# Split matmuls of a decoder layer with the moving columns and the PSUM columns taken in descending order

## The chip, the cores and the metric

The kernel runs on one core of one Trainium2 chip. The metric is the device time of one execution in microseconds. The kernel before was run three times: 1579.78, 1580.56 and 1582.54 us, median 1580.56 us. The profile is of one further execution.

## What is computed

One layer of a hybrid decoder, for 256 prompt tokens and 8 single-token samples together (264 columns), model width 2048, feed-forward width 5632:

```python
def layer(x, ...):
    xn = rmsnorm(x, g_mix)
    z = xn @ w_in                                  # 2048 x 5128
    y_rg = ...                                     # causal conv, gated linear recurrence
    y_ml = ...                                     # chunked mLSTM, 4 heads
    x = x + jnp.concatenate([y_rg, y_ml], axis=-1) @ w_out
    xq = (rmsnorm(x, g_xa) @ w_xa_q).reshape(B, L, XA_HEADS, XA_DH)
    s = jnp.einsum('blhd,bmhd->bhlm', xq, mk) * (XA_DH ** -0.5)
    p = jax.nn.softmax(s, axis=-1)
    o = jnp.einsum('bhlm,bmhd->blhd', p, mv).reshape(B, L, D_MODEL)
    x = x + o @ w_xa_o
    xf = rmsnorm(x, g_ffn)
    x = x + (jax.nn.silu(xf @ w_ffn_gate) * (xf @ w_ffn_up)) @ w_ffn_down
    return x
```

The memory keys and values `mk`, `mv` come from `rmsnorm(mem) @ w_xa_k` and `@ w_xa_v` for the prompt (256 memory tokens) and from a cache for the samples. All inputs and outputs are fp32. Beside the tokens' outputs the new recurrent states and the prompt's memory keys and values are returned.

## The kernel before

Activations stand transposed: 128 features on the partitions, 264 tokens along the free dimension, 16 chunks of 128 features for the model width. Every projection is cut into **steps** (the list `steps`). A step takes one weight piece of 128 x 2048 fp32 (1 MB), makes one output block of 128 features x 264 tokens and, in the common case, runs over 16 chunks of the contraction.

To get fp32 accuracy from a single pass, each fp32 operand is split into two tiles of type fp32r: a high part (ScalarE copies and so rounds it) and a low part (VectorE subtracts the high part from the original). The weights are split so in `split_half`, half a piece at a time, into tiles `wh` and `wl`; the activations are split once, when they are made, into two tiles out of the pool `B`. `mm3` then makes a product as the sum of three matmuls into the same PSUM bank: high weight by high activation, high weight by low activation, low weight by high activation. A matmul's second argument is the stationary operand (128 columns), the third the moving operand, whose columns stream through the array; the first is the PSUM output.

`mm3` is called at six places:

- `proj`: 16 (12 in the last part of the down projection) calls a step; n is 264, or 256 for the memory keys.
- `pe_first`: the first four pieces of `w_in`, into four banks at a time, 264 columns.
- `pe_o`: the output projection of the cross attention, 264 columns (two lines of it, 1108 to 1118).
- `attend`: scores (line 1046) and weighted values (line 1079) of the prompt's cross attention, 256 columns, in banks with the tag `ax`.

Other matmuls do not go through `mm3` and stay as they are: `pe_v` (the memory values, 512 columns, the memory activations stationary and the weights moving), the plain fp32 matmuls of the recurrence and the mLSTM, the sums over tokens, the spreading of a factor over the partitions, and the transposes.

PSUM has four banks with the tag `mm` and four with the tag `ax`, each 512 fp32 wide; an output takes columns 0 to 263 (or 0 to 255) of its bank, and a moving operand is a contiguous row of 264 (or 256) fp32 in its tile.

The order of the work: the main loop goes through the steps, issues the DMA of the piece three steps ahead (SyncE queue), the split of the piece one step ahead, the step's matmuls, and then as much of the side work (recurrence, mLSTM, attention, norms) as its own price list says will fit. A tile scheduler places the semaphore waits. Between writes of TensorE itself to one PSUM bank it also sets waits of TensorE on its own semaphore where it sees need.

Of the kernel before, what the change touches and what calls it, by code (L numbers as in the profile page):

```python
# [80 lines left out]
def layer_kernel(ctx: ExitStack, tc, xT, memT, vec, wrg, w_in, w_out, w_q, w_k, w_v, w_o,  # L81
# [92 lines left out]

    def mm3(ps, a, b, start, stop):
        ah, al = a
        bh, bl = b
        pe.matmul(ps, ah, bh, start=start, stop=False)
        pe.matmul(ps, ah, bl, start=False, stop=False)
        pe.matmul(ps, al, bh, start=False, stop=stop)  # L180
# [609 lines left out]
    def proj(src, rhs, evac, cols=2048, n=N, need=()):  # L790

        def f(i):
            ps = bank()
            w = W(i)
            nch = cols // P
            for c in range(nch):
                mm3(ps[:, :n], w(c), rhs(c), c == 0, c == nch - 1)
            return ps
        steps.append((src, cols, f, evac, need))
# [5 lines left out]
    def pe_first(q):  # L805
        def f(i):
            w = W(i)
            for n in range(4):
                for c in range(4):
                    mm3(first[n][:, :N], w(4 * n + c), rx(4 * q + c), q + c == 0, q + c == 6)  # L810
        return f
# [220 lines left out]
    def attend(h):  # L1032
# [9 lines left out]
        for tb in range(2):  # L1042
            ps = bank("ax")
            s = slice(tb * P, tb * P + P)
            for c in range(4):
                mm3(ps[:, :T], (qh[:, c, s], ql[:, c, s]), K(c), c == 0, c == 3)
            yield STEP
            mx, su = sm[:, 2 * tb: 2 * tb + 1], sm[:, 2 * tb + 1: 2 * tb + 2]
            dve.tensor_reduce(mx, ps[:, :T], axis=AX.X, op=OP.max)
            dve.tensor_scalar(mx, mx, -XSCALE, None, op0=OP.mult)  # L1050
            act.activation(p[:, tb, :], ps[:, :T], AF.Exp, scale=XSCALE, bias=mx, accum_out=su)
            yield 0.5
# [147 lines left out]
    for i, (src, cols, pef, evf, need) in enumerate(steps):  # L1200
# [17 lines left out]
        ps = pef(i)  # L1218
# [127 lines left out]
```

## Time and profile before

| what | value |
|---|---|
| runs, median of three | 1580.56 us (1579.78 to 1582.54) |
| profiled execution, span from first to last instruction | 1577.6 us |
| median less span | 2.96 us |
| TensorE (PE) busy | 1560.9 us, 99%, 12356 matmuls |
| weight load (PEld) busy | 1536.0 us, 97%, 12356 loads |
| VectorE (DVE) busy | 1047.3 us, 66% |
| ScalarE (ACT) busy | 779.2 us, 49% |
| GpSimd (POOL) busy | 74.9 us, 5% |
| DMA | 325.97 MB, mean 207 GB/s |
| TensorE's mean granted clock | 0.994 of full speed |

The profile gives no separate time of its execution, only the span, so the span is what a sum is made against; the median of the runs lies 2.96 us above it. The line number of nearly all instructions is that of a helper (line 60), so groups are told apart by tile names and shapes: `mm<-B,wh 128x264` is a matmul into a bank with the tag `mm`, with an activation tile of pool `B` moving and the high half of the weights stationary. The time that the profile gives for one matmul contains its way through the array, and neighbours overlap; how often matmuls start is read from their number in a stretch of time.

### The profile page before, as it was taken

To read this page: it belongs to the slowest core of one execution; us is meant where nothing else is said; L and a number is where in the kernel's file an instruction comes from. 1 tells how busy PE (TensorE), PEld (TensorE's weight loads), DVE (VectorE), ACT (ScalarE), POOL (GpSimd) and SP (SyncE) were. 2 spreads that over 40 slices of the span, in tenths; PEclk is the share of its full clock that TensorE was granted. 3 is DMA by queue.
4 is the path that set the end of the run, shared out by engine and by line. 5 is a ranking of instruction groups with operands and counts; after the bars stand their busy time and mean duration, and the time that the engine had idled before them with its cause. 6 is when DMAs were issued, how large, how long until landed. Compare 5 with 4: busy or idle time off the path is not lost.

```text
span 1577.6 us, 29752 instructions
## 1 busy us (share of the span) xinstructions
PE 1560.9 (99%) x12356; PEld 1536.0 (97%) x12356; DVE 1047.3 (66%) x2019; ACT 779.2 (49%) x1217; POOL 74.9 (5%) x142
## 2 busy tenths in 40 slices
PE   9999999999999999999999999999999999999997
PEld 9999999999999889989999999999999999999997
DVE  7976878787689999856655555455555554555554
ACT  7465775564445555545444444333444433344463
POOL 0001210001012112000000000000000000000000
PEclk9999999999999999999999999999999999999999
DMA  8445875547689888554545555455445555555452
GB/s 311 154 174 171 303 262 202 189 159 260 247 298 353 314 330 302 178 182 180 187 163 185 188 181 173 182 187 186 174 178 185 188 181 174 180 188 188 153 180 97
DMA packets 55303, 325.97 MB, mean 207 GB/s; under 512 B 6688, under 2 KB 7120, under 8 KB 24448
## 3 DMA queue, kind: packets, MB, share of 16 engines
q1 hardware_dynamic: 39744, 270.68, 47.9%
q0 software_dynamic: 15136, 53.16, 9.2%
q8 instruction: 96, 1.57, 0.4%
q10 hardware_dynamic: 288, 0.23, 0.1%
q14 instruction: 39, 0.32, 0.1%
HBM read 312.78 MB, written 11.28 MB: 205 GB/s over the span
## 4 chain that ended last, share of the span: by engine, by line
PE 97%; ACT 1%; DVE 1%; DMA 0%; issue 0%; SPq 0%; DVEq 0%; ACTq 0%
PE mm L60 92%; PE ax L60 6%; DVE B L60 1%; ACT B L60 1%; DMA xres<-xT 0%; ACT wh L60 0%; ACT L60 0%; DVE wl L60 0%; DVE c L60 0%; DVEq L1323 0%; DVE xres L60 0%; ACT t L60 0%; SPq L1185 0%; ACT rstd L60 0%; SPq L1178 0%
## 5 line engine op out<-in xcount | busy, mean ns | idle before, releaser
L60 PE MATMUL mm<-B,wh 128*128 128x264 f32 (+1 forms) x7520 | 1380.0, 285 | 2.8 <-DVE B L60 2.8
L60 PEld LDWEIGHTS mm<-B,wh 128*128 128x128 f32 x7520 | 1166.8, 189 | 4.4 <-ACT cso L60 2.9
L60 PE MATMUL mm<-B,wl 128*128 128x264 f32 (+1 forms) x3760 | 1066.9, 284 | 1.2 <-DVE wl L60 1.2
L60 ACT ACTIVATE wh<-raw 128x1024 fp32r<-128x1024 f32 (+2 forms) x518 | 538.4, 1041 | 710.1 <-PE mm L60 584.1
L60 DVE TENSOR_TENSOR wl<-raw,wh 128x1024 fp32r<-128x1024 f32 (+2 forms) x518 | 620.7, 1200 | 370.0 <-ACT wh L60 361.8
L60 PEld LDWEIGHTS mm<-B,wl 128*128 128x128 f32 x3760 | 708.8, 189 | 1.6 <-DVE wl L60 1.4
L60 DVE TENSOR_TENSOR t<-mm,rstd 128x264 f32<-128x264 f32 x104 | 44.9, 432 | 57.5 <-PE mm L60 57.5
L60 PE MATMUL mm<-wh,B 128*128 128x512 f32 x256 | 83.0, 398 | 0.0
L60 DVE TENSOR_TENSOR xres<-xres,mm 128x264 f32<-128x264 f32 x80 | 34.3, 428 | 46.5 <-PE mm L60 46.5
L60 PEld LDWEIGHTS mm<-wh,B 128*128 128x128 f32 x256 | 48.4, 189 | 10.5
L60 DVE SCALAR_TENSOR_TENSOR dw<-B,dw 128x256 f32<-128x256 f32 x128 | 53.8, 420 | 3.2 <-ACT dw L60 2.2
L60 PE MATMUL mm<-wl,B 128*128 128x512 f32 x128 | 51.0, 398 | 0.0
L60 PE MATMUL ax<-B,B 128*128 128x256 f32 (+3 forms) x288 | 48.7, 312 | 0.0
L60 DVE SCALAR_TENSOR_TENSOR dw<-B,qsm,dw 128x256 f32<-128x256 f32 x96 | 45.9, 480 | 1.2 <-ACT dw L60 0.6
L60 PEld LDWEIGHTS ax<-B,B 128*128 128x128 f32 x288 | 40.7, 189 | 3.4 <-issue 0.7
L1238 POOL TENSOR_TENSOR B<-B,rstd 128x264 f32<-128x264 f32 x4 | 2.8, 739 | 866.0 <-ACT rstd L60 866.0
L60 ACT ACTIVATE B<-xres,vecs 128x264 fp32r<-128x264 f32 (+1 forms) x64 | 31.2, 504 | 2.5 <-DMA xres<-xT 1.3
L60 ACT ACTIVATE t<-xres 128x264 f32<-128x264 f32 x60 | 23.8, 416 | 15.3 <-DVE xres L60 15.3
L60 PEld LDWEIGHTS mm<-wl,B 128*128 128x128 f32 x128 | 24.1, 188 | 5.1
L936 POOL DMA_DIRECT2D B<-kcT x32 | 17.3, 541 | 209.9 <-DVE B L60 119.3
L60 DVE TENSOR_TENSOR acc_x<-acc_x,t 128x264 f32<-128x264 f32 x59 | 25.3, 428 | 0.8 <-ACT t L60 0.5
L60 DVE SCALAR_TENSOR_TENSOR B<-xres,vecs,B 128x264 fp32r<-128x264 f32 x48 | 22.7, 489 | 4.5 <-ACT B L60 4.5
(152 smaller groups left out, 701.3 us busy)
## 6 DMA issues: line engine op xcount, KB each, us to landing
raw<-w_gu SPq DMA_DIRECT2D x88, 1024.0 KB, 4.8
raw<-w_in SPq DMA_DIRECT2D x40, 1024.0 KB, 4.8
raw<-w_d SPq DMA_DIRECT2D x32, 1024.0 KB, 4.8
raw<-w_out SPq DMA_DIRECT2D x16, 1024.0 KB, 4.8
B<-kcT POOLq DMA_DIRECT2D x32, 512.0 KB, 7.0
raw<-w_q SPq DMA_DIRECT2D x16, 1024.0 KB, 6.6
B<-vcT POOLq DMA_DIRECT2D x32, 512.0 KB, 7.6
raw<-w_k SPq DMA_DIRECT2D x16, 1024.0 KB, 7.2
```

The costliest lines, as they stand in the source:

```text
L60: return f(*a, **k)
L936: pool_e.dma_start(kc, kcT[h, b])
L1238: e.tensor_mul(st["y"](c), st["y"](c), r)
```

## The change

In `mm3` the output and both parts of the moving operand are taken with a step of -1 along their free dimension. Element k of the output still comes from element k of the moving operand; only the order in which the columns are read and written is turned round. The stationary operand, the number of matmuls, their shapes, the flags and all other matmuls are the same, and whoever reads the PSUM bank afterwards reads it in ascending order as before.

```diff
     def mm3(ps, a, b, start, stop):
         ah, al = a
-        bh, bl = b
+        ps, bh, bl = ps[:, ::-1], b[0][:, ::-1], b[1][:, ::-1]
         pe.matmul(ps, ah, bh, start=start, stop=False)
         pe.matmul(ps, ah, bl, start=False, stop=False)
         pe.matmul(ps, al, bh, start=False, stop=stop)
```

The order of the instructions on every engine stays as it was. What does differ is on which instructions TensorE waits for its own semaphore (`PE_49`): there are 24 such matmuls before and 41 now, and four ScalarE instructions have one more wait on TensorE. The first place is TensorE at the head of a step of `w_in` (the bank `mm_3771` is taken for a new output):

```order
 L60 MATMUL mm_3698<-B_3492,wh_3629 128x264 [waits DVE_49]
 L60 MATMUL mm_3698<-B_3491,wl_3630 128x264
-L60 MATMUL mm_3771<-B_3330,wh_3690 128x264
+L60 MATMUL mm_3771<-B_3330,wh_3690 128x264 [waits PE_49]
 L60 MATMUL mm_3771<-B_3331,wh_3690 128x264
 L60 MATMUL mm_3771<-B_3330,wl_3691 128x264
```

Nothing moved; the first matmul into the bank got a wait on TensorE's own earlier work. The second place is TensorE in the cached attention of the samples (`dw` by `ones` sums over partitions) and the prompt's scores behind it (`ax_7137`, through `mm3`):

```order
 L60 MATMUL mm_7053<-wl_7107,B_4249 128x512
 L60 MATMUL mm_7053<-wh_7106,B_4250 128x512
-L60 MATMUL ax_7084<-dw_7032,ones 128x256 [waits DVE_49]
-L60 MATMUL ax_7137<-B_6763,B_7080 128x256
+L60 MATMUL ax_7084<-dw_7032,ones 128x256 [waits DVE_49,PE_49]
+L60 MATMUL ax_7137<-B_6763,B_7080 128x256 [waits PE_49]
 L60 MATMUL ax_7137<-B_6764,B_7080 128x256
 L60 MATMUL ax_7137<-B_6763,B_7081 128x256
```

Again the order is the same and two matmuls have a wait more.

## Prediction

> **What bounds the kernel now.** I read the page first, for which engine is never idle. Its head, its busy shares, the slices of TensorE and its clock, and the chain that ended last:
>
> ```profile
> span 1577.6 us, 29752 instructions
> PE 1560.9 (99%) x12356; PEld 1536.0 (97%) x12356; DVE 1047.3 (66%) x2019; ACT 779.2 (49%) x1217; POOL 74.9 (5%) x142
> PE   9999999999999999999999999999999999999997
> PEclk9999999999999999999999999999999999999999
> PE 97%; ACT 1%; DVE 1%; DMA 0%; issue 0%; SPq 0%; DVEq 0%; ACTq 0%
> ```
>
> TensorE is busy in every slice but the last, at full clock, and 97% of the chain is TensorE. So the time is the number of matmuls times the distance between their starts, and whatever the change does to that distance arrives in the time almost undiminished. A busy TensorE does not say how fast it goes, so next I asked for the matmuls by shape, for their number and the duration of one:
>
> ```profile
> L60 PE MATMUL mm<-B,wh 128*128 128x264 f32 x7008 | 1286.5, 285 | 2.8 <-DVE B L60 2.8
> L60 PE MATMUL mm<-B,wl 128*128 128x264 f32 x3504 | 994.9, 284 | 1.2 <-DVE wl L60 1.2
> L60 PE MATMUL ax<-B,wh 128*128 128x264 f32 x64 | 13.5, 308 | 1.9 <-ACT wh L60 1.4 <-ACT B L60 0.3
> L60 PE MATMUL ax<-B,wl 128*128 128x264 f32 x32 | 9.4, 304 | 0.0
> L60 PE MATMUL mm<-B,wh 128*128 128x256 f32 x512 | 93.5, 283 | 0.0
> L60 PE MATMUL mm<-B,wl 128*128 128x256 f32 x256 | 72.0, 281 | 0.0
> L60 PE MATMUL ax<-B,B 128*128 128x256 f32 x216 | 34.6, 300 | 0.0
> L60 PE MATMUL mm<-wh,B 128*128 128x512 f32 x256 | 83.0, 398 | 0.0
> ```
>
> The first four rows are all `mm3` at 264 columns: 7008 + 3504 + 64 + 32 = 10608, which is 221 steps of 48. The next two are the memory keys, 768 at 256 columns. Of the 216 in the seventh row, 192 are `mm3` in `attend` (4 heads, 24 for the scores and 24 for the values); the rest belong to the mLSTM. So 10608 + 960 = **11568** matmuls of the 12356 are touched. The last row, 512 columns, is `pe_v`, which is untouched; it serves as a price.
>
> The 285 ns of one matmul are not its distance from the next. For that I took busy times by stretches (the columns are the stretch, its length, busy time and count of PE, clock, DMA share, GB/s). The first row is the long feed-forward stretch, where only 264-column `mm3` runs; the last is the beginning:
>
> ```profile
> 807.20:1563.00 755.80, 755.80 (x6233) 1.00 0.50 176
> 0.00:206.00 206.00, 199.01 (x1496) 0.97 0.65 227
> ```
>
> 755.80 us / 6233 = **121.3 ns** from start to start. Is that distance a matter of what else runs, or of which buffers are used? The same view in four equal stretches, with the other engines (PE, PEld, DVE, ACT, POOL, then clock and DMA):
>
> ```profile
> 700.00:900.00 200.00, 200.00 (x1655) 200.00 (x1654) 118.66 (x170) 92.96 (x129) 1.08 (x2) 1.00 0.51 180
> 900.00:1100.00 200.00, 200.00 (x1651) 200.00 (x1650) 106.83 (x123) 79.69 (x88) 0.00 (x0) 1.00 0.50 181
> 1100.00:1300.00 200.00, 200.00 (x1653) 200.00 (x1651) 109.85 (x133) 82.64 (x97) 0.00 (x0) 1.00 0.51 180
> 1300.00:1500.00 200.00, 200.00 (x1653) 200.00 (x1652) 108.15 (x129) 80.98 (x96) 0.00 (x0) 1.00 0.51 177
> ```
>
> Between 1651 and 1655 in 200 us, though the activations lie in other buffers in each stretch (the residual's, then each part's products). The mean distance thus is the same to 0.24% whatever the addresses.
>
> **The price of a column.** Two steps of `pe_v` follow the memory keys directly; the timeline around their first and their last matmul:
>
> ```profile
> 672.35 0.40 PE L60 MATMUL mm<-wh,B 128*128 128x512 f32 x1
> 672.59 0.39 PE L60 MATMUL mm<-wl,B 128*128 128x512 f32 x1
> ...
> 683.26 0.40 PE L60 MATMUL mm<-wh,B 128*128 128x512 f32 x1
> ```
>
> Two steps are 48 matmuls, so 47 distances in 683.26 - 672.35 = 10.91 us: 232.1 ns for 512 columns. Between 264 and 512 columns one column costs (232.1 - 121.3) / 248 = **0.447 ns**; 264 of them make 118.0 ns, and 3.3 ns of the 121.3 do not depend on the columns. So nearly the whole distance is streaming of columns, which is just what the change touches.
>
> **The change, part by part.** Nothing is removed or added: the instruction lists of all engines are the same, the same 11568 matmuls with the same weights, and no DMA moves. Three things change.
>
> (a) **Descending reads and writes.** The trace has no row with a descending operand, so I bound its cost by the nearest rows. At the lower side, if the 3.3 ns that do not depend on columns went away, 11568 x 3.3 ns = 38 us would be gained: 1542. If such a start-up were paid twice, 38 us would be lost: 1619. At the upper side, if a descending column took two column slots instead of one, a 264-column matmul would stand like one of 528 columns: 264 x 0.447 = 118.0 ns more, and a 256-column one 114.4 ns more. 10608 x 118.0 ns = 1251.7 us, 960 x 114.4 ns = 109.8 us, in sum 1361.5 us. Between these ends I take **0**, the row the operand is nearest to: the steady stretch itself. The columns are the same ones, neighbours stay neighbours, and both widths are even, so two neighbours that shared an aligned 8 bytes when counted from column 0 share them when counted from column 263 or 255; and the four stretches show no dependence of the mean on where the operands lie.
>
> [...]
>
> (b) **Waits of TensorE on itself.** 41 matmuls have one, 24 had one. What such waits cost today is in the list of TensorE's waits, which is complete with six rows:
>
> ```profile
> PE mm L60 <- DVE B L60: 2.8, 1, 2.8
> PE ax L60 <- ACT wh L60: 1.4, 1, 1.4
> PE mm L60 <- DVE wl L60: 1.2, 1, 1.2
> PE mm L60 <- DVE ones L60: 1.1, 1, 1.1
> PE ax L60 <- ACT B L60: 0.3, 1, 0.3
> PE mm L60 <- DVE c L60: 0.3, 1, 0.3
> ```
>
> No idle time is put down to TensorE itself, so the 24 cost nothing that shows. Each waits for an older writer of the same bank; four banks are in turn, so that writer mostly lies steps (of 48 x 121.3 ns = 5.8 us) back. The bound for the 17 more: each waits out one matmul in flight, 285 - 121 = 164 ns, 2.8 us in all. Behind such a matmul every later matmul queues, and behind those VectorE and ScalarE with the next output; but I take 0, since the cover is the steps between. If that cover were gone it would be the 2.8 us.
>
> (c) **The four waits on ScalarE.** They stand on the exponentials of the prompt's scores, which already wait for VectorE's maximum over the same bank; that maximum was itself behind TensorE's write, so the new wait is over before the old one. 0.
>
> The sum is 0 us against the span of 1577.6 us. The median of the runs lies 2.96 us above the span, and so the forecast is that median, 1580.6, rounded to **1581 us**. The small terms, (b) and the start-up of (a), give this case its own range, 1561 (half of the 38 us gained) to 1619.
>
> **The rivals.**
>
> *Two slots per column.* The place is the stream of 11568 matmuls; it decides as soon as either the read of the moving row or the write of the bank can handle neighbours together only in ascending order. In its favour: a column at 0.447 ns is the fastest thing in this trace. One fp32 of VectorE's subtraction, in the row below, takes 1225 / 1024 = 1.20 ns, so TensorE's stream moves a column 2.7 times as fast, which may well rest on taking two together.
>
> ```profile
> L60 DVE TENSOR_TENSOR wl<-raw,wh 128x1024 fp32r<-128x1024 f32 x496 | 606.9, 1225 | 369.2 <-ACT wh L60 361.0 <-PE mm L60 0.9
> ```
>
> Against it: the pairs stay whole. The price: 1361.5 us, less what TensorE now loses to waits at the beginning, since a slower TensorE hides those. The first 206 us hold 1496 matmuls, which at 121.3 ns would take 181.5 us, so 24.5 us go. 1580.6 + 1361.5 - 24.5 = **2918 us**. [...] With the slope of the durations instead, (398 - 285) / 248 = 0.456 ns, and nothing hidden, it is 1580.6 + 10608 x 120.4 ns + 960 x 116.7 ns = 2970.
>
> *A small cost at each start.* A descending row may need another start or meet the weight loads differently. In the place of 3.3 ns, up to 6.6: 1581 to 1619, slower. The loads are hidden as long as their turn comes within the distance between matmuls; PEld is busy 97% and shows equal counts, so the trace does not say how much room is left.
>
> *A small gain* by the same route: down to 1542. For it speaks only that the 3.3 ns exist.
>
> *The change does nothing at all*, because both sides of the copy are turned and the two could cancel: 1581. The view of the order prints shapes alone and can't exclude it; the different waits show at least that the scheduler sees other access patterns.
>
> *Worse than two slots*, for instance four because reads and writes both break and don't overlap: beyond 2970.
>
> **How the numbers follow.** The forecast (same stream, no start-up that can be told, the cancelled change included): 0.39. Small cost 0.13, small gain 0.10, two slots 0.33, worse 0.05. About 0.2% is what a measurement of this kernel can tell from no change. Faster is 0.10, same 0.39, slower 0.13 + 0.33 + 0.05 = 0.51: the likeliest single case is no change, while the slower cases together outweigh it. The near cases hold 0.62 only, so the range must take in two slots: from 1561, which leaves out half of the small gain, to 2970, which leaves out the worse case; 0.10 is left out.
>
> **What would show it.** In the profile after, the steady stretch decides: about 6233 matmuls in 755.8 us if I am right, about 3160 (239.3 ns apart) with two slots. In the latter case the 512-column matmuls must stay at 232.1 ns, VectorE's and ScalarE's busy times stay, and their shares fall. A start-up cost would show in the 264- and 256-column distance by equal nanoseconds, a slot cost in proportion to the columns. For (b) the list of TensorE's waits should show no new row of weight, and a row with TensorE waiting for itself would prove it wrong. The prediction is wrong if descending order costs the stream anything per column.

## The result

The changed kernel takes 1583.73 us (median of 7 runs, 1582.98 to 1588.14) against 1580.56 us before (7 runs, 1579.17 to 1582.54). The ratio is **1.0023, 95% interval [1.0014, 1.0033]**: 2.2 to 5.2 us slower. The stream of matmuls did not go to two slots a column; something of 0.2% was added. The profiled execution after is the slowest of its seven (span 1586.4 us), so its span is no measure of the 3 us; its steady stretches are.

The page after, the same lines as before:

```profile
span 1586.4 us, 29758 instructions
PE 1569.4 (99%) x12356; PEld 1544.4 (97%) x12356; DVE 1047.6 (66%) x2019; ACT 778.3 (49%) x1217; POOL 74.6 (5%) x142
PEclk9999999999999999999999999999999999999999
PE 96%; DVE 1%; ACT 1%; DMA 1%; issue 0%; DVEq 0%; SPq 0%; ACTq 0%
```

Only PE and PEld have grown, by 8.5 and 8.4 us, with the same 12356 instructions; VectorE and ScalarE do what they did (1047.6 us against 1047.3, 778.3 against 779.2). By shape:

```profile
L60 PE MATMUL mm<-B,wh 128*128 128x264 f32 x7008 | 1292.7, 286 | 2.8 <-DVE B L60 2.8
L60 PE MATMUL mm<-B,wl 128*128 128x264 f32 x3504 | 1002.2, 286 | 1.1 <-DVE wl L60 1.1
L60 PE MATMUL mm<-B,wh 128*128 128x256 f32 x512 | 93.8, 284 | 0.0
L60 PE MATMUL mm<-wh,B 128*128 128x512 f32 x256 | 83.0, 398 | 0.0
```

A 264-column matmul lasts 286 ns where it lasted 284 or 285; the untouched 512-column one has not moved (398 ns). For the distance between starts I count matmuls in one stretch of 600 us, all of it feed-forward, first in the kernel before and then after (stretch, length, busy time and count of PE, clock, DMA share, GB/s):

```profile
900.00:1500.00 600.00, 600.00 (x4952) 1.00 0.51 180
```

```profile
900.00:1500.00 600.00, 600.00 (x4935) 1.00 0.51 180
```

17 fewer in 600 us at the same clock, 0.34% (0.42 ns a matmul in this stretch). Over the whole trace, the mean distance between neighbouring `mm3` matmuls of 264 columns, taken from the starts of their rows, is 121.26 ns before and 121.60 ns after (pairs over 140 ns apart, where something else lies between, left out). 10608 x 0.34 ns = 3.6 us, which is the size of the median's 3.2 us.

The list of TensorE's waits after is again six rows, and none waits for TensorE:

```profile
PE mm L60 <- DVE B L60: 2.8, 1, 2.8
PE ax L60 <- ACT wh L60: 1.2, 1, 1.2
PE ax L60 <- DVE B L60: 1.2, 1, 1.2
PE mm L60 <- DVE ones L60: 1.1, 1, 1.1
PE mm L60 <- DVE wl L60: 1.1, 1, 1.1
PE mm L60 <- DVE c L60: 0.3, 1, 0.3
```

Of the rest of the profiled span's 8.8 us, some 3 us are at one place that the page's clock line, in tenths, hides. The stretch from 235 to 250 us, before and then after:

```profile
235.00:250.00 15.00, 15.00 (x128) 1.00 0.92 342
```

```profile
235.00:250.00 15.00, 15.00 (x102) 0.77 0.85 316
```

In this execution TensorE's granted clock was 0.77 on average there: 26 matmuls fewer, 26 x 121 ns = 3.1 us. Narrowed to where it happens, 6.8 us stand at half clock:

```profile
241.10:247.90 6.80, 6.80 (x33) 0.50 1.01 405
```

The remaining 1 to 2 us arise ahead of 206 us, where the list above has a wait for VectorE of 1.2 us (`PE ax L60 <- DVE B L60`) that the profile before lacks. The same wait of 1.2 us stands in two profiles with ascending operands (64 bytes more in the weight tiles, and step 2, below), so the change does not bring it.

### The profile page after: what moved, and what is told of

It reads as the page before. It is cut to its first block, busy times and chain, and to the rows that moved or that the text cites. A ratio compares the mean times of both kernels' runs of the same rounds, so it can differ in the third digit from the quotient of the medians.

```text
span 1586.4 us, 29758 instructions
## 1 busy us (share of the span) xinstructions
PE 1569.4 (99%) x12356; PEld 1544.4 (97%) x12356; DVE 1047.6 (66%) x2019; ACT 778.3 (49%) x1217; POOL 74.6 (5%) x142
## 4 chain that ended last, share of the span: by engine, by line
PE 96%; DVE 1%; ACT 1%; DMA 1%; issue 0%; DVEq 0%; SPq 0%; ACTq 0%
PE mm L60 91%; PE ax L60 5%; DVE B L60 1%; DMA o_sc<-B 1%; ACT B L60 0%; DMA raw<-w_in 0%; DVE wl L60 0%; ACT wh L60 0%; ACT L60 0%; DVE t L60 0%; DVE c L60 0%; DVEq L1323 0%; DVE xres L60 0%; ACT t L60 0%; ACT rstd L60 0%
## 5 line engine op out<-in xcount | busy, mean ns | idle before, releaser
L60 PE MATMUL mm<-B,wh 128*128 128x264 f32 (+1 forms) x7520 | 1386.4, 286 | 2.8 <-DVE B L60 2.8
L60 PEld LDWEIGHTS mm<-B,wh 128*128 128x128 f32 x7520 | 1172.1, 189 | 4.4 <-ACT cso L60 2.9
L60 PE MATMUL mm<-B,wl 128*128 128x264 f32 (+1 forms) x3760 | 1074.2, 286 | 1.1 <-DVE wl L60 1.1
L60 ACT ACTIVATE wh<-raw 128x1024 fp32r<-128x1024 f32 (+2 forms) x518 | 537.4, 1039 | 716.9 <-PE mm L60 591.3
L60 DVE TENSOR_TENSOR wl<-raw,wh 128x1024 fp32r<-128x1024 f32 (+2 forms) x518 | 620.9, 1200 | 370.8 <-ACT wh L60 363.2
L60 PEld LDWEIGHTS mm<-B,wl 128*128 128x128 f32 x3760 | 710.1, 189 | 1.5 <-DVE wl L60 1.3
L60 DVE TENSOR_TENSOR t<-mm,rstd 128x264 f32<-128x264 f32 x104 | 44.9, 432 | 61.2 <-PE mm L60 61.2
L60 PE MATMUL mm<-wh,B 128*128 128x512 f32 x256 | 83.0, 398 | 0.0
L60 DVE TENSOR_TENSOR xres<-xres,mm 128x264 f32<-128x264 f32 x80 | 34.3, 429 | 46.5 <-PE mm L60 46.5
L60 PEld LDWEIGHTS mm<-wh,B 128*128 128x128 f32 x256 | 48.3, 189 | 10.5
L60 DVE SCALAR_TENSOR_TENSOR dw<-B,dw 128x256 f32<-128x256 f32 x128 | 53.9, 421 | 3.2 <-ACT dw L60 2.2
L60 PE MATMUL mm<-wl,B 128*128 128x512 f32 x128 | 50.9, 398 | 0.0
L60 PE MATMUL ax<-B,B 128*128 128x256 f32 (+3 forms) x288 | 48.9, 313 | 1.2 <-DVE B L60 1.2
L60 DVE SCALAR_TENSOR_TENSOR dw<-B,qsm,dw 128x256 f32<-128x256 f32 x96 | 46.0, 481 | 1.2 <-ACT dw L60 0.6
L60 PEld LDWEIGHTS ax<-B,B 128*128 128x128 f32 x288 | 40.8, 189 | 4.7 <-issue 2.3
L60 ACT ACTIVATE B<-xres,vecs 128x264 fp32r<-128x264 f32 (+1 forms) x64 | 31.1, 502 | 3.0 <-DMA xres<-xT 1.5
L60 ACT ACTIVATE t<-xres 128x264 f32<-128x264 f32 x60 | 23.7, 413 | 15.2 <-DVE xres L60 15.2
L60 PEld LDWEIGHTS mm<-wl,B 128*128 128x128 f32 x128 | 24.1, 188 | 5.1
L60 DVE SCALAR_TENSOR_TENSOR B<-xres,vecs,B 128x264 fp32r<-128x264 f32 x48 | 22.7, 490 | 4.9 <-ACT B L60 4.9
L60 DVE TENSOR_TENSOR acc_x<-acc_x,t 128x264 f32<-128x264 f32 x59 | 25.3, 429 | 0.8 <-ACT t L60 0.5
```

The lines of the kernel that those rows point to most:

```text
L60: return f(*a, **k)
```

## The experiments

What had to be told apart: is the third of a nanosecond due to the descending **read** of the moving operand, the descending **write** of PSUM, or the added **waits**? And is it a price of the direction, or of the addresses that the reads then take? The theories are named in the expectations. All ratios are to runs of the kernel before on the same chip.

### One half of the change at a time

```diff
 read_only
-        bh, bl = b
+        bh, bl = b[0][:, ::-1], b[1][:, ::-1]
 write_only
-        bh, bl = b
+        ps, bh, bl = ps[:, ::-1], b[0], b[1]
```

Read alone. 

> Only the two moving operands of the split matmuls descend; the output ascends, so every product comes out with its columns mirrored (the result is not the layer's). Theory A (the distance between matmuls depends on where the SBUF reads start, and descending only draws other addresses): the steady feed-forward stretch stands at 121.6 ns as with the whole change, total 1583.7, +3 us. Theory B (a descending PSUM write costs a little at each start): 121.3 ns, 1580.6, no change. Theory C (the added waits of TensorE on itself cost the 3 us): 1580.6, since the waits come from the output's pattern.

Write alone. 

> Only the PSUM output of the split matmuls descends; the moving operands ascend, so the products come out mirrored (the result is not the layer's). Theory A: steady distance 121.3 ns, total 1580.6, no change. Theory B: 121.6 ns, 1583.7. Theory C: 1583.7 with the steady distance at 121.3 ns and the 3 us in the list of TensorE's waits.

The same stretch of 600 us, read alone and then write alone:

```profile
900.00:1500.00 600.00, 600.00 (x4935) 1.00 0.51 179
```

```profile
900.00:1500.00 600.00, 600.00 (x4951) 1.00 0.51 179
```

Read alone has the 4935 of the whole change (mean distance over the whole trace 121.60 ns), write alone has the count of before less one (121.27 ns). Total times: 1583.98 us, ratio 1.0019 [1.0007, 1.0032], for the read; 1578.28 us, ratio 0.9983 [0.9974, 0.9992], for the write. So theories B and C fall: the descending write costs the stream nothing that shows (121.27 against 121.26 ns), and neither do the waits, which come from the write. The write alone is even 0.17% faster, which no theory expected. Its stream is not: taken in blocks of 480 split matmuls, its distances stay within 0.07 ns of those before. In the profiles its lead arises ahead of 140 us, where the kernel before has a stretch at half clock that the write alone has not (first before, then write alone):

```profile
120.00:140.00 20.00, 18.81 (x130) 0.83 0.47 160
```

```profile
120.00:140.00 20.00, 18.84 (x152) 1.00 0.49 159
```

Over all runs on that chip its mean granted clock was 0.9952 (11 runs) against 0.9937 (30 runs) before. The difference of 0.0015 makes 2.4 us of 1580, which is the size of the 2.2 us between the medians. So the lead goes with the clock; why the clock was granted more in these runs, they do not show.

### Moving everything by 32 bytes

```diff
+    pad = const.tile([P, 4], F32, name="pad")
+    pool_e.memset(pad, 0.0)
     ident = const.tile([P, P], F32, name="ident")
```

Ascending. 

> The kernel before (ascending), with an unused constant of 4 columns ahead of everything, which moves all SBUF tiles behind it by 32 bytes. Theory A: the distances within a step take another pattern, and their mean moves by some tenths of a ns either way (1577 to 1584.5). Theories B and C: 121.3 ns, 1580.6.

Descending. 

> The whole change (descending), with the same 32 bytes of shift. Theory A: again another pattern, its mean some tenths of a ns from 121.6 either way and not bound to lie above that of the ascending kernel with the same shift. Theory B: 0.33 ns above the ascending one with the same shift, 3.5 us in the total. Theory C: 3 us above it, in waits.

(Four fp32 are 16 bytes; the tiles behind them start 32 bytes later, as the expectations say.) The kernel before with the shift, then the change with it:

```profile
900.00:1500.00 600.00, 600.00 (x4951) 1.00 0.50 180
```

```profile
900.00:1500.00 600.00, 600.00 (x4935) 1.00 0.50 179
```

Means 121.27 and 121.59 ns; totals 1579.52 us, ratio 0.9993 [0.9984, 1.0001], and 1583.80 us, ratio 1.0022 [1.0011, 1.0032]. Theory A as I had put it was wrong: a shift of all tiles together changes nothing. What stood then was either a fixed price of a descending row (theory E) or the place of the moving reads *relative to the weight loads*, which this shift leaves alone (theory D).

### Moving the weights against the activations

```diff
 asc_wpad, desc_wpad (1032); asc_wpad64, desc_wpad64 (1040)
-        wh = sb.tile([P, 1024], F32R, tag="wh", bufs=4, name=nm("wh"))
-        wl = sb.tile([P, 1024], F32R, tag="wl", bufs=4, name=nm("wl"))
+        wh = sb.tile([P, 1032], F32R, tag="wh", bufs=4, name=nm("wh"))
+        wl = sb.tile([P, 1032], F32R, tag="wl", bufs=4, name=nm("wl"))
```

32 bytes a buffer, ascending. 

> The kernel before (ascending) with 8 unused columns at the end of each weight tile, which moves the four buffers of each kind by 32 to 128 bytes against the activations and against each other. If the 0.33 ns of the descending read come from how its addresses meet those of the weight loads (theory D), the mean distance of the 264-column matmuls leaves 121.27 ns by some tenths either way. If a descending row just starts later (theory E), it stays at 121.27.

32 bytes, descending. 

> The whole change (descending) with the same 8 unused columns in the weight tiles. Theory D: the mean distance leaves 121.60 ns, and may fall below that of the ascending kernel with the same tiles. Theory E: 121.60 ns, 0.33 above it.

64 bytes, ascending. 

> The kernel before with 16 unused columns in each weight tile (buffers moved by 64 bytes and its multiples). Theory D (addresses of the activations against those of the weight loads): a third draw, 120.9 to 122 ns for 264 columns, and the total follows at 10.6 us per ns, 1577 to 1589. Theory E (start of a descending row): 121.27 ns, 1580.5.

64 bytes, descending. 

> The whole change with the same weight tiles. Theory D: a draw of its own, 120.9 to 122 ns, above or below the ascending one with these tiles. Theory E: 121.60 ns, 1584, 0.33 ns above the ascending one.

The stretch of 600 us in these four, in the same order:

```profile
900.00:1500.00 600.00, 600.00 (x4924) 1.00 0.51 179
```

```profile
900.00:1500.00 600.00, 600.00 (x4927) 1.00 0.51 179
```

```profile
900.00:1500.00 600.00, 600.00 (x4941) 1.00 0.51 179
```

```profile
900.00:1500.00 600.00, 600.00 (x4932) 1.00 0.52 179
```

| weight tiles | read | 264 columns, ns | 256 columns, ns | total, us (ratio) |
|---|---|---|---|---|
| as before | ascending | 121.26 | 117.91 | 1580.56 |
| as before | descending | 121.60 | 118.34 | 1583.73 (1.0023) |
| + 32 bytes | ascending | 121.68 | 118.47 | 1587.66, one run |
| + 32 bytes | descending | 121.68 | 117.72 | 1582.71, one run |
| + 64 bytes | ascending | 121.58 | 118.06 | 1582.96 (1.0017 [1.0008, 1.0026]) |
| + 64 bytes | descending | 121.64 | 118.01 | 1585.20 (1.0022 [1.0012, 1.0033]) |

(The distances are means between neighbouring starts over each whole trace, pairs over 140 ns apart left out.) Theory E falls. With 32 bytes more in the weight tiles the two directions stand equally far apart at 264 columns on average, and at 256 the descending one is 0.75 ns closer, which a fixed price of a descending row can't give. With 64 bytes the ascending kernel, without any descending operand, is as slow as the change within the intervals. The traces of the kernel before and of the change say the same without any shift. In the stretch behind the memory values, the same number of 264-column matmuls takes 66.50 us ascending and 66.30 us descending:

```profile
715.80:782.30 66.50, 66.50 (x551) 1.00 0.52 186
```

```profile
722.70:789.00 66.30, 66.30 (x551) 1.00 0.53 187
```

Taken in blocks of 480 split matmuls, the change stands between 0.28 ns nearer and 0.91 ns farther apart than the kernel before, depending on the block, and the read alone repeats this block by block to 0.02 ns.

Theory D, that the distance goes by where the reads and the weights lie, is what is left. Each activation tile holds four chunks. In the 600 us of the kernel before, the matmuls of the first, second, third and fourth chunk start 121.96, 121.69, 120.86 and 120.43 ns behind the matmul ahead of them. With everything moved by 32 bytes these four numbers stay to 0.02 ns; with the change they are 122.55, 120.98, 121.73 and 121.32. The two edits of the weight tiles also move these against each other: with 32 bytes more, the four `wh` buffers move by 0 to 96 bytes, the four `wl` buffers behind them by 128 to 224 (not 32 to 128, as the expectation has it), and the small tiles behind these by 256. That the reads count in relation to the weights therefore rests on both together: the change turns round the reads alone, and its effect differs with the place of the weights. So 121.26 ns was the best of the six combinations at 264 columns, and the change left it as both shifts of the weights did. Which relation of addresses makes a good one, the runs do not show.

The two single runs differ by 5 us in favour of descending at equal distances. The ascending one has a stretch at half clock, as the change's profile had, which is worth 3 of the 5; first the ascending one, then the descending one over a longer stretch round the same place:

```profile
238.30:245.10 6.80, 6.80 (x34) 0.50 1.03 414
```

```profile
230.00:250.00 20.00, 20.00 (x170) 1.00 0.80 290
```

That half-clock stretch near 240 us does not hang on the descending read. Of the profiles taken, 4 of 6 with a descending read and 4 of 8 with an ascending one have it. It follows 18 matmuls of one column (plain fp32 sums of the side work), which fill 2 us with hardly a column streamed:

```profile
238.31 2.06 PE L60 MATMUL ax<-ones,B 128*128 128x1 f32 x18
...
241.05 0.60 PE L60 MATMUL mm<-B,wh 128*128 128x264 f32 x2
```

From the second row on (the change's profile), a pair takes 0.60 us in place of 0.41. In each trace the clock changes on a grid of 3.41 us: in the kernel before, the stretches from one change to the next last 3.41, 6.83, 37.55 and 75.09 us, which are 1, 2, 11 and 22 steps of it. In the eight profiles that have the stretch, the 18 matmuls begin 0.2 to 1.0 us behind a point of that grid; in the six that have not, five begin 1.3 to 2.9 us behind one, and the sixth 0.5 us. That speaks for the 18 matmuls as what sets it off, but no run without them was taken, so it is not shown. The stretch of 6.8 us is two steps of the grid.

### What would have broken the stream

Why did two slots not come? The 768 matmuls of the memory keys were given moving operands of 256 columns that are not neighbours, or not an aligned pair:

```diff
-    rm = lambda c: st["mem"](c)
+    def rm(c):
+        return st["mem"](c)
+
+    def rk(c):
+        q, o = divmod(c, 4)
+        o = min(o, 2) * T
+        v = lambda t: t.tile(q).rearrange("p a b -> p (a b)")[:, o: o + 2 * T: 2]
+        return v(st["mem"].h), v(st["mem"].l)
...
-            proj(w_k[4 * h + j], rm, evac_k(h, j), n=T, need=("memg",))
+            proj(w_k[4 * h + j], rk, evac_k(h, j), n=T, need=("memg",))
```

(`rm` does what it did and stays for the values. With a step of 4: `o = 0` and `[:, 0: 4 * T: 4]`. The odd start: `o = min(o, 2) * T + 1` and `[:, o: o + T]`, in the kernel before and in the change.)

Step 2. 

> The kernel before, but the 768 matmuls of the memory keys read their moving operand with a step of 2 columns (8 bytes) over two neighbouring chunks, 256 columns as before, so the memory keys and what follows from them are other numbers (the work is the same). If TensorE takes two columns together as long as they lie in one line of 16 bytes, the distance stays at 117.9 ns and the total at 1580. If it can take two together only from neighbouring addresses, in whichever order, they stand 114 ns further apart (232 ns) and the total grows by 768 x 114 ns = 88 us to 1668.

Step 4. 

> As the run with a step of 2, but with a step of 4 columns (16 bytes) over four chunks: every column in another line of 16 bytes (the memory keys are other numbers). If two columns of one line are what gives the speed, this is where the two-slot price appears: 232 ns and 1668 us. If neither order nor step matters to the read, 117.9 ns and 1580.

Odd start, ascending. 

> The kernel before, but the 768 matmuls of the memory keys read 256 columns that begin at an odd column of their tile (one column further, so the memory keys are other numbers). If two columns are taken together only as an aligned 8 bytes, every pair is broken: 232 ns and 1668 us, as with a step of 2. If any two neighbours will do, about 118 ns and 1580.

Odd start, descending. 

> The whole change, and the memory keys read in descending order from an even column down to an odd one, so that again no pair is an aligned 8 bytes (the memory keys are other numbers). Aligned pairs needed: 232 ns, 1671. Any two neighbours in either order: about 118 ns, 1584.

The same run of 110 matmuls of the memory keys, with no other between, in the kernel before, the change, step 2, step 4, odd ascending and odd descending:

```profile
596.13:609.15 13.02, 13.02 (x111) 1.00 0.88 287
```

```profile
602.79:615.86 13.07, 13.07 (x111) 1.00 0.87 279
```

```profile
647.44:672.53 25.09, 25.09 (x111) 1.00 0.35 119
```

```profile
647.18:672.74 25.56, 25.56 (x111) 1.00 0.33 117
```

```profile
597.88:611.35 13.47, 13.47 (x111) 1.00 0.85 280
```

```profile
598.50:611.82 13.32, 13.32 (x111) 1.00 0.84 273
```

The stretches go from the first start to just behind the last, so each holds 109 distances (the count of 111 has the neighbour at the edge): 119.4 ns before, 119.9 with the change, **230.2 with a step of 2, 234.5 with a step of 4**, 123.6 and 122.2 from an odd column. A step of 2 costs 110.8 ns a matmul, close to the 114.4 ns that the prediction had worked out for two slots, and the totals follow: 1665.51 us, ratio 1.0537 [1.0514, 1.0560], and 1670.16 us, ratio 1.0555 [1.0528, 1.0581]. The odd starts give 1582.37 and 1584.67 us in one run each. The two slots were an estimate of mine; the runs show that the distance nearly doubles with a step of 2 or 4, and not how that comes about. With a step of 2 the 117.9 ns of the first case in its expectation did not come, and a start at an odd column costs only 2 to 4 ns a matmul (123.6 against 119.4 ascending, 122.2 against 119.9 descending).

On the side of PSUM the descending write stands at 121.27 ns against 121.26. A PSUM output with a step of 2, or one that begins at an odd column, wasn't tried.

## Why the prediction came out as it did

- **What bounds it.** TensorE's distance between starts sets the time: held. 0.34 ns of it came back as some 3 us in the total.
- **(a) Descending reads and writes, taken as 0.** It measured 0.34 ns for 264 columns and 0.43 ns for 256: 10608 x 0.34 + 960 x 0.43 = 4.0 us, inside the measured 2.2 to 5.2. The write's part is 0, as taken. The argument that pairs stay neighbours gave the right answer. That an aligned 8 bytes counts was my assumption, and no run shows it: an odd start, which breaks every such pair, costs 2 to 4 ns a matmul where two slots were priced at 114.4. Of the two signs that the prediction named, neither came: the added distance is not equal at both widths, and it is larger at the smaller width, so it is no price per column. That its mean is as small as 0.34 ns is in part luck, since it runs from -0.28 to 0.91 ns by blocks.
- **The step that was off by this term** is "no dependence of the mean on where the operands lie", read from four stretches that agree to 0.24%. In all four the weight tiles lay in the same eight buffers, and 0.24% is itself as large as the effect. A mean over whole steps also hides what goes on in them, from 120.43 to 121.96 ns by chunk. Moving only the weight tiles and the small ones behind them took the ascending kernel from 121.26 to 121.68 ns.
- **(b) and (c), waits at 0.** Held: no new row in TensorE's list waits for TensorE, and the read alone, which has no new waits, is as slow as the whole.
- **Two slots a column, at 2918 us.** Did not happen with a step of -1, which added 0.34 ns. A step of 2 added 110.8 ns, of the 114.4 that were priced. It had been given 0.33, on no run: what spoke for it was the speed of a column, 0.447 ns, and that two are taken together there is not shown.
- **A small cost at each start, 1581 to 1619.** The size came, not the mechanism: a cost of the descending row would be there with any weight tiles, and it is 0.00 and 0.06 ns at 264 columns and -0.75 and -0.05 ns at 256 with the two others.
- **The change does nothing at all.** Excluded by the read alone, which takes another distance.
- **The forecast of 1581** was 2.7 us low. The ratio of 1.0023 is just above the 0.2% that the prediction took as the least that can be told, and its interval leaves out no change at all. That 1583.73 lies in a range of 1561 to 2970 says little by itself, since the range was stretched to take in two slots.

## What to carry to other kernels

Turning the moving columns and the PSUM columns of these matmuls round cost 0.2%, and that by the place of the tiles; stepping over columns of the moving operand about doubled the distance (119.4 to 230.2 ns at 256 columns), so lay it out contiguously before it comes to TensorE. Here the time is one distance times ten thousand, and moving the weight tiles, with the small ones behind them, took that distance from 121.26 to 121.58 and 121.68 ns, 0.3% as with the change itself; such an effect must be told from the change's own by moving the tiles in both kernels. When the span of a single profile disagrees with the medians, look for a stretch at half clock before explaining it (here 6.8 us at 0.50, worth 3.1 us).

## What the runs showed of the hardware that I had not expected

- An fp32r moving operand with a step of 2 columns streams at 230.2 ns for 256 columns against 119.4 ns contiguous; a step of 4 is hardly worse (234.5 ns).
- Descending order runs at the contiguous rate to 0.4% on both sides (121.60 against 121.26 ns with the read descending, 121.27 with the write), and an operand that begins at an odd column runs within 4.2 ns of it (123.6 against 119.4 ns ascending, 122.2 against 119.9 descending).
- The distance between matmuls went with where the tiles lie in relation to each other: 121.26 to 121.68 ns at 264 columns and 117.72 to 118.47 at 256 with three places of the weight tiles and both directions, and 121.27 ns again after a shift of all tiles together by 32 bytes.
